# Compression weights split by VectorE, and the compression's steps moved in the filler list of a hybrid attention block

## The chip, the cores and the metric

One core of one Trainium2 chip runs the whole program. The metric is device time in microseconds from launch to end. Three runs of the kernel before gave 636.03, 636.63 and 637.7 us; the median is 636.63 us.

Five engines work in parallel, each through its own instructions in order: TensorE (PE; its weight loads are shown as PEld), VectorE (DVE), ScalarE (ACT), GpSimd (POOL), and SyncE (SP), which here only starts transfers. An instruction that waits holds up all that stands behind it on its engine.

## The reference

The input x is 512 tokens by 1024. The block does, in this order:

- h = rms_norm(x); u = h @ w_in. The columns of u are queries, three pairs of keys and values, head gates, and three times 512 columns for a gated convolution (b, c, x_t).
- Attention of 8 heads (2 groups) in three branches. For the compressed one, windows of 32 keys (values) at stride 16 go through a two-layer network: `gelu(blk @ w1) @ w2`, 31 compressed keys and values per group. The other two branches are the selected blocks and the sliding window. Each branch has a bias, a softmax and a gate.
- A convolution branch: b * dwconv3(c * x_t).
- Both are joined, multiplied by w_out, normed and added to x. A gated MLP with a width-3 convolution (2 x 2816 columns up, 2816 rows down) follows in the same way.

All of it is float32.

## The kernel before

**Exact products from two halves.** Every operand X of a large matmul is kept as hi = X rounded to the matmul's type, and lo = X - hi. A product takes three matmuls: hi*hi, hi*lo, lo*hi (`mm3`, L169). For the weights, `Stream._split` makes both halves: ACT copies the raw tile to hi (L85), another engine subtracts to get lo (L88). That engine is DVE, except for the tiles named in `pool_lo`: there it is POOL, in four pieces of 256 columns (L81 to L88). Before, `pool_lo` holds the eight tiles `c1_0` to `c1_7`, the weights of the compression's first layer (L167).

**The weight stream.** Weight tiles of 128 x 1024 come in one fixed order, that in which the filler list first names them. Raw tiles have three buffers: a load waits until the raw tile three places earlier has been split. Split tiles have four buffers (`ringp`, L119): the hi copy of a tile waits until TensorE has used the tile four places earlier for the last time. Splits carry a raised priority (L96).

**The filler list.** After the startup, TensorE's work is of two sorts. One is attention, in 14 parts (`Part`: scores, exp, transposes, products with the values), each of which needs DVE and ACT between its matmuls. The other is filler, which needs no softmax: `ORDER` (L44) is a list of steps, and `fill(n)` takes the next n steps of it. The names: `c`, `q` are projections for compressed keys/values and queries; `h0` to `h7` are the first layer of the compression (two steps each: 16 matmuls of 256 columns, weight `c1_n`); `s` is `second_layer` in three steps (L462); `g`, `x`, `b` with 0 to 3 are the convolution's three projections of one 128-channel tile, eight steps of three 512-column matmuls each. So `g0:2` is two steps of gate projection 0.

**What sets the counts.** All filler up to the last `s` step (`PRE2`, L154) is placed ahead of the first attention part's second half, because the compressed scores (`pcs`) need the second layer's result. What is left (`TOTAL - PRE2`) is spread over the twelve parts that follow (L711). The framework's scheduler then orders each engine's instructions by priority and readiness, so the order on an engine is not that of the source.

**The second layer**, step one: ACT copies half of the accumulator `ph` to `g1` (L467), DVE adds the other half (L468). Step two: TensorE transposes `g1` into `pg` (L472), ACT applies gelu to get `GT`, which needs a table load (L481), DVE copies it to `GV`. Step three: TensorE multiplies by `w2` (`pc`, `pvc`), the results are split to `KC` and `VC`, and `KC` is copied to the other partitions by a transfer.

**A convolution tile**: g gives `cz` (DVE), x multiplies it (DVE, L532), POOL scales it (two pieces, L519), POOL and DVE apply the three taps to get `ct` (L535, L537), POOL scales again (L519), b multiplies (DVE, L544), and ACT and DVE split it into `oTc` (L134, L135).

Of the kernel before, what the change touches and what calls it, by code (L numbers as in the profile page):

```python
# [40 lines left out]
BIG = 1e30  # L41


ORDER = ("c0 c1 q2 q3:4 h0 q3:4 h1 g0:2 h2 g0:2 h3 g0:2 h4 g0:2 h5 x0:4 h6 x0:4 h7 s:1 b0:3 s:1 b0:3 s:1 b0:2 "  # L44
         "g1 x1 b1 g2 x2 b2 g3 x3 b3")
LOADS = "g w", "T0 T1 T2 w T3 T4 b T5 w T6 T7 w", "x0 x1 v x2 x3 w"
T_TILES = 20
WARM = 8
# [62 lines left out]
def block_kernel(ctx: ExitStack, tc: tile.TileContext, a, out):  # L111
# [28 lines left out]
    c1 = lambda c: (a["w_c1"][c].rearrange("p l c -> p (l c)"), 1024, f"c1_{c}")  # L140
# [7 lines left out]
    order = []  # L148
    for what in ORDER.split():
        name, _, count = what.partition(":")  # L150
# [13 lines left out]
    items += [(a["w_d"][f * P:(f + 1) * P, :], 1024, f"d{f}") for f in range(NF)]  # L164
    W = Stream(tc, nc, rawp, ringp, items, loads=0)
    W.pieces["v0"] = 280
    W.pool_lo |= {f"c1_{c}" for c in range(8)}  # L167

    def mm3(dst, wh, wl, xh, xl, first, last):  # L169
        MM(dst, wh, xh, start=first, stop=False)  # L170
# [583 lines left out]
    x1 = late.tile([P, NT, D], F32, name="x1")  # L754
# [104 lines left out]
    for n, m in enumerate(UP):  # L859
# [7 lines left out]
        if m >= NF:  # L867
            f = m - NF
# [97 lines left out]
```

## Time and profile before

| | |
|---|---|
| median of three runs | 636.63 us |
| profiled execution, its own time | 636.99 us |
| its span, first to last instruction | 635.2 us |
| TensorE busy | 622.5 us (98%) |
| VectorE / ScalarE / GpSimd busy | 368.4 / 306.3 / 71.7 us |
| mean granted TensorE clock | 0.992 of 2.4 GHz |

The page's own note says that a busy TensorE is not one at its peak: matmuls overlap in the pipeline, so the start of one to the start of the next is the pace, not the duration shown. The program has four stretches: startup up to some 43 us, filler and the first part to about 113 us, attention with filler to about 222 us, and then the output projection and the MLP.

### The profile page before, as it was taken

The page shows a single profiled execution, that of the slowest core. Times are in us where ns is not written, and L with a number is a line of the kernel's source. Part 1 is how long each engine was busy: PE and PEld are TensorE (multiplying, and loading weights), DVE is VectorE, ACT ScalarE, POOL GpSimd, SP SyncE. Part 2 cuts the span into 40 slices and gives each one's busy share as a digit, 9 for nine tenths or more (in the row PEclk, how much of TensorE's full clock was granted, in tenths as well). Part 3 has the DMA queues.
Part 4 walks back from the last instruction along what each step waited for, and adds up shares of the span by engine and source line. Part 5 has one row for each costly group of instructions (what it writes and reads, how often), then busy time and mean ns, then how long its engine had stood idle before and what let it go on. Part 6 is the DMA issues. An engine that isn't in the chain of part 4 may idle for free.

```text
span 635.2 us, 8091 instructions
## 1 busy us (share of the span) xinstructions
PE 622.5 (98%) x2980; PEld 518.7 (82%) x2980; DVE 368.4 (58%) x657; ACT 306.3 (48%) x562; POOL 71.7 (11%) x122
## 2 busy tenths in 40 slices
PE   8999997999999999999999999999999999999996
PEld 7888895888878788898888888888888888888884
DVE  5686625799978756638665656565656642222225
ACT  6666634789878744436343444444444422222212
POOL 1204383002230302200000000000000000000001
PEclk9999997999999999999999999999999999999998
DMA  8876455111121474004233233322222232232203
GB/s 324 322 208 185 130 180 166 43 43 42 42 76 42 152 269 165 11 1 135 99 99 101 99 100 99 101 100 98 90 88 96 93 111 92 97 100 99 67 0 133
DMA packets 26294, 71.44 MB, mean 112 GB/s; under 512 B 3368, under 2 KB 8040, under 8 KB 26256
## 3 DMA queue, kind: packets, MB, share of 16 engines
q1 hardware_dynamic: 25968, 70.65, 33.6%
q8 instruction: 23, 0.38, 0.2%
q10 hardware_dynamic: 288, 0.29, 0.1%
q14 instruction: 15, 0.12, 0.1%
HBM read 64.88 MB, written 2.12 MB: 105 GB/s over the span
## 4 chain that ended last, share of the span: by engine, by line
PE 82%; DMA 5%; DVE 4%; ACT 3%; POOL 3%; issue 2%; SPq 1%; DVEq 0%; POOLq 0%; ACTq 0%
PE pu L171 13%; PE pu L170 13%; PE pu L172 13%; PE z L770 6%; PE z L772 6%; PE z L771 6%; PE tr L650 3%; PE sc L621 2%; PE y L772 2%; PE y L770 2%; PE y L771 2%; POOL w_c L88 2%; DMA raw_tb<-in_w_t 2%; PE o L658 2%; PE o L659 1%
## 5 line engine op out<-in xcount | busy, mean ns | idle before, releaser
L170 PE MATMUL pu<-h2T,w_u 128*128 128x512 f32 (+1 forms) x384 | 142.8, 372 | 0.0
L171 PE MATMUL pu<-h2T,w_u 128*128 128x512 f32 (+1 forms) x384 | 142.6, 371 | 0.0
L172 PE MATMUL pu<-h2T,w_u 128*128 128x512 f32 (+1 forms) x384 | 142.6, 371 | 0.0
L170 PEld LDWEIGHTS pu<-h2T,w_u 128*128 128x128 f32 x384 | 72.4, 188 | 12.6
L172 PEld LDWEIGHTS pu<-h2T,w_u 128*128 128x128 f32 x384 | 72.3, 188 | 12.5
L171 PEld LDWEIGHTS pu<-h2T,w_u 128*128 128x128 f32 x384 | 72.4, 188 | 12.3
L854 DVE SCALAR_TENSOR_TENSOR cv<-pu,ffnw,cv 128x511 f32<-128x511 f32 x44 | 32.9, 749 | 70.2 <-ACT cv L853 70.2
L88 DVE TENSOR_TENSOR w_d<-raw_d,w_d 128x1024 fp32r<-128x1024 f32 x22 | 26.9, 1224 | 72.8 <-ACT w_d L85 72.8
L771 PE MATMUL z<-w_d,aT 128*128 128x512 f32 x176 | 68.5, 389 | 0.0
L770 PE MATMUL z<-w_d,aT 128*128 128x512 f32 x176 | 68.5, 389 | 0.0
L772 PE MATMUL z<-w_d,aT 128*128 128x512 f32 x176 | 68.5, 389 | 0.0
L853 ACT ACTIVATE cv<-pu,ffnw 128x512 f32<-128x512 f32 x44 | 30.3, 688 | 63.7 <-PE pu L172 63.6
L85 ACT ACTIVATE w_d<-raw_d 128x1024 fp32r<-128x1024 f32 x22 | 23.3, 1059 | 75.2 <-PE z L772 75.2
L88 DVE TENSOR_TENSOR w_u<-raw_u,w_u 128x1024 fp32r<-128x1024 f32 x44 | 53.4, 1216 | 5.8 <-ACT w_u L85 5.8
L85 ACT ACTIVATE w_u<-raw_u 128x1024 fp32r<-128x1024 f32 x44 | 46.2, 1052 | 6.5 <-PE pu L172 6.3
L254 POOL TENSOR_SCALAR rsz<-ssz 128x1 f32<-128x1 f32 x4 | 1.2, 300 | 355.0 <-ACT jz L893 355.0
L627 ACT ACTIVATE P<-P,mins 128x512 f32<-128x512 f32 (+3 forms) x64 | 35.4, 555 | 10.1 <-DVE mins L625 9.7
L772 PEld LDWEIGHTS z<-w_d,aT 128*128 128x128 f32 x176 | 33.0, 188 | 6.9
L771 PEld LDWEIGHTS z<-w_d,aT 128*128 128x128 f32 x176 | 33.0, 188 | 6.9
L770 PEld LDWEIGHTS z<-w_d,aT 128*128 128x128 f32 x176 | 33.0, 188 | 6.8
L134 ACT ACTIVATE aT<-cv 128x512 fp32r<-128x512 f32 x22 | 13.9, 632 | 49.5 <-DVE cv L871 49.5
L855 DVE SCALAR_TENSOR_TENSOR cv<-pu,ffnw,cv 128x510 f32<-128x510 f32 x44 | 32.8, 748 | 1.5
(222 smaller groups left out, 1165.0 us busy)
## 6 DMA issues: line engine op xcount, KB each, us to landing
raw_u<-in_w_u SPq DMA_DIRECT2D x44, 512.0 KB, 3.2
raw_d<-in_w_d SPq DMA_DIRECT2D x22, 512.0 KB, 3.2
raw_c<-in_w_c SPq DMA_DIRECT2D x8, 512.0 KB, 3.4
raw_o<-in_w_o SPq DMA_DIRECT2D x8, 512.0 KB, 3.3
xT<-in_xT SPq DMA_DIRECT2D x8, 256.0 KB, 5.4
xt<-in_x SPq DMA_DIRECT2D x4, 512.0 KB, 5.9
raw_q<-in_w_t SPq DMA_DIRECT2D x4, 512.0 KB, 6.6
UR<-vd SPq DMA_DIRECT2D x2, 1024.0 KB, 8.7
```

Source lines behind the costliest of these rows:

```text
L85: self.nc.scalar.activation(t[:, 0, c:c + step], self.raws[n][:, c:c + step], AF.Copy)
L88: eng.tensor_tensor(t[:, 1, cs], self.raws[n][:, cs], f32(t[:, 0, cs]), op=ALU.subtract)
L170: MM(dst, wh, xh, start=first, stop=False)
L171: MM(dst, wh, xl, start=False, stop=False)
L172: MM(dst, wl, xh, start=False, stop=last)
L627: act(v, v, AF.Exp, bias=m, scale=-1.0, accum_out=self.sums[:, r, b:b + 1])
L770: MM(y, oh_, w[:, 0, cs], start=first, stop=False)
L771: MM(y, ol_, w[:, 0, cs], start=False, stop=False)
L772: MM(y, oh_, w[:, 1, cs], start=False, stop=last)
L853: act(t, pu, AF.Copy, scale=ffnw[:, m, 2:3])
L854: nc.vector.scalar_tensor_tensor(t[:, 1:], pu[:, :S - 1], ffnw[:, m, 1:2], t[:, 1:], op0=ALU.mult, op1=ALU.add)
L855: nc.vector.scalar_tensor_tensor(t[:, 2:], pu[:, :S - 2], ffnw[:, m, 0:1], t[:, 2:], op0=ALU.mult, op1=ALU.add)
```

## The change

`c1_0` to `c1_7` are no longer in `pool_lo`, so their lo halves are made by DVE, in one instruction of 1024 columns each instead of four POOL instructions of 256. And `ORDER` is rewritten: the first layer's `h2` to `h7` stand four projection steps apart each (before: two steps apart for `h2` to `h5`, then four), with `g0`, `x0` and all of `b0` between them; and the second layer's three steps stand between steps of `g1` (before: of `b0`). The second layer comes after 82 list steps instead of 73, so the twelve parts that follow share 65 steps instead of 74.

```diff
@@ -41,8 +41,8 @@
-ORDER = ("c0 c1 q2 q3:4 h0 q3:4 h1 g0:2 h2 g0:2 h3 g0:2 h4 g0:2 h5 x0:4 h6 x0:4 h7 s:1 b0:3 s:1 b0:3 s:1 b0:2 "
-         "g1 x1 b1 g2 x2 b2 g3 x3 b3")
+ORDER = ("c0 c1 q2 q3:4 h0 q3:4 h1 g0:4 h2 g0:4 h3 x0:4 h4 x0:4 h5 b0:4 h6 b0:4 h7 s:1 g1:4 s:1 g1:3 s:1 g1:1 "
+         "x1 b1 g2 x2 b2 g3 x3 b3")
@@ -164,7 +164,6 @@
     W.pieces["v0"] = 280
-    W.pool_lo |= {f"c1_{c}" for c in range(8)}
```

One line less stands ahead of most of the code, so line numbers after the change are one smaller.

ScalarE, where the second layer begins, before: the hi copies of the next weights (`w_tg1`, `w_tx1`, `w_tb1` are gate, x and b of channel tile 1), then the copy to `g1`.

```order
L85 ACTIVATE w_c1_7_934<-raw_c1_7_877 128x1024
L85 ACTIVATE w_tb0_954<-raw_tb0_896 128x1024
L85 ACTIVATE w_tg1_988<-raw_tg1_923 128x1024
L85 ACTIVATE w_tx1_1007<-raw_tx1_940 128x1024
L85 ACTIVATE w_tb1_1276<-raw_tb1_957 128x1024
L467 ACTIVATE g1_1003<-ph_759 64x512
L481 ACT_TABLE_LOAD
L481 ACTIVATE GT_1026<-pg_1021,peb_1028 128x2x31 x4
```

The same place on ScalarE after the change:

```order
L85 ACTIVATE w_c1_7_952<-raw_c1_7_888 128x1024
L85 ACTIVATE w_tg1_969<-raw_tg1_905 128x1024
L85 ACTIVATE w_tx1_997<-raw_tx1_941 128x1024
L85 ACTIVATE w_tb1_1016<-raw_tb1_955 128x1024
L134 ACTIVATE oTc_511<-ct0_932 128x512
L466 ACTIVATE g1_1012<-ph_753 64x512
L85 ACTIVATE w_tg2_1279<-raw_tg2_972 128x1024
L480 ACT_TABLE_LOAD
L480 ACTIVATE GT_1038<-pg_1033,peb_1040 128x2x31 x4
```

The copy to `g1` still stands behind the hi copies of `w_tx1` and `w_tb1`, and now also behind the split of the finished convolution tile 0.

VectorE at the same place, before:

```order
L88 TENSOR_TENSOR w_tx1_1007<-raw_tx1_940,w_tx1_1007 128x1024
L537 SCALAR_TENSOR_TENSOR ct0_982<-cz0_914,convw_290,ct0_982 128x512
L468 TENSOR_TENSOR g1_1003<-ph_759,g1_1003 64x512
L537 SCALAR_TENSOR_TENSOR ct0_982<-cz0_914,convw_290,ct0_982 128x512
L478 COPY peb_1028<-pg_1021 128x4
```

And after:

```order
L88 TENSOR_TENSOR w_c1_7_952<-raw_c1_7_888,w_c1_7_952 128x1024
L88 TENSOR_TENSOR w_tg1_969<-raw_tg1_905,w_tg1_969 128x1024
L536 SCALAR_TENSOR_TENSOR ct0_932<-cz0_868,convw_290,ct0_932 128x512 x2
L88 TENSOR_TENSOR w_tx1_997<-raw_tx1_941,w_tx1_997 128x1024
L543 TENSOR_TENSOR ct0_932<-pbg0_951,ct0_932 128x512
L88 TENSOR_TENSOR w_tb1_1016<-raw_tb1_955,w_tb1_1016 128x1024
L135 TENSOR_TENSOR oTc_511<-ct0_932,oTc_511 128x512
L467 TENSOR_TENSOR g1_1012<-ph_753,g1_1012 64x512
```

Ahead of the addition to `g1` now stand the product with b0 (L543), the lo half of `w_tb1` and that of `oTc`. On TensorE, the transposes `pg` of `g1` stood behind `h7` and 13 matmuls of `b0`; now they stand behind `h7` and 12 matmuls of `g1`.

## Rows read from the trace of the kernel before

**Rows 1.** The page: the span, and busy time, share and instructions of each engine.

```profile
span 635.2 us, 8091 instructions
PE 622.5 (98%) x2980; PEld 518.7 (82%) x2980; DVE 368.4 (58%) x657; ACT 306.3 (48%) x562; POOL 71.7 (11%) x122
```

**Rows 2.** TensorE's waits, 0 to 260 us: total, times, longest, us.

```profile
PE pg L472 <- DVE g L468: 3.9, 1, 3.9
```

**Rows 3.** TensorE in order of time: start us, us, [idle before].

```profile
87.72 0.39 PE L170 MATMUL pxt<-hT,w_tx 128*128 128x512 f32 x1
...
90.48 1.84 PE L458 MATMUL ph<-w_c,X 128*128 128x256 f32 x8
92.16 0.40 PE L170 MATMUL pxt<-hT,w_tx 128*128 128x512 f32 x1
...
99.29 0.39 PE L170 MATMUL pbg<-hT,w_tb 128*128 128x512 f32 x1
103.56 0.69 PE L472 MATMUL pg<-ident,g 64*128 64x64 f32 x4 [3.88 <-DVE g L468]
```

**Rows 4.** Stretches of 2 us: busy of PE, PEld, DVE, ACT, POOL; clock; DMA.

```profile
102.00:104.00 2.00, 0.44 (x4) 0.45 (x4) 1.18 (x2) 1.96 (x3) 0.00 (x0) 0.64 0.49 186
104.00:106.00 2.00, 2.00 (x7) 1.54 (x6) 1.88 (x4) 1.01 (x5) 1.69 (x2) 0.50 0.01 2
106.00:108.00 2.00, 2.00 (x6) 1.32 (x4) 1.06 (x2) 0.00 (x0) 0.91 (x2) 0.50 0.62 213
108.00:110.00 2.00, 2.00 (x7) 1.07 (x7) 0.00 (x0) 0.20 (x1) 0.00 (x0) 0.66 0.12 49
```

**Rows 5.** ScalarE in order of time, ahead of the second layer.

```profile
101.11 1.06 ACT L85 ACTIVATE w_tb<-raw_tb 128x1024 fp32r<-128x1024 f32 x1 [2.11 <-DMA raw_tb<-in_w_t]
102.19 0.59 ACT L467 ACTIVATE g<-ph 64x512 f32<-64x512 f32 x1
```

**Rows 6.** VectorE in order of time, the same place.

```profile
93.81 1.83 DVE L88 TENSOR_TENSOR w_tb<-raw_tb,w_tb 128x1024 fp32r<-128x1024 f32 x1 [6.81 <-ACT w_tb L85]
...
97.19 0.68 DVE L532 TENSOR_TENSOR cz<-pxt,cz 128x512 f32<-128x512 f32 x1
99.03 1.24 DVE L88 TENSOR_TENSOR w_tx<-raw_tx,w_tx 128x1024 fp32r<-128x1024 f32 x1 [1.16 <-ACT w_tx L85]
100.87 0.75 DVE L537 SCALAR_TENSOR_TENSOR ct<-cz,convw,ct 128x512 f32<-128x512 f32 x1 [0.59 <-POOL ct L535]
102.82 0.68 DVE L468 TENSOR_TENSOR g<-ph,g 64x512 f32<-64x512 f32 x1 [1.20 <-ACT g L467]
...
104.36 1.22 DVE L88 TENSOR_TENSOR w_tb<-raw_tb,w_tb 128x1024 fp32r<-128x1024 f32 x1
```

**Rows 7.** GpSimd in order of time, the same place.

```profile
91.74 2.82 POOL L88 TENSOR_TENSOR w_c<-raw_c,w_c 128x256 fp32r<-128x256 f32 x4 [1.12 <-ACT w_c L85]
97.95 1.24 POOL L519 TENSOR_TENSOR cz<-cz,Rb 128x256 f32<-128x256 f32 x2 [3.39 <-DVE cz L532]
99.29 1.54 POOL L535 TENSOR_SCALAR ct<-cz,convw 128x512 f32<-128x512 f32 x1
...
104.38 2.54 POOL L519 TENSOR_TENSOR ct<-ct,Rb 128x256 f32<-128x256 f32 x2
```

**Rows 8.** Tile oTc, 90 to 135 us: duration ns min/median/max, starts.

```profile
L135 DVE TENSOR_TENSOR oTc<-ct,oTc x1: 678/678/678, 132.8 to 132.8; 128x512 fp32r<-128x512 f32 x1
```

**Rows 9.** The DMA queue's waits, 40 to 115 us: total, times, longest, us.

```profile
SPq L73 <- POOL w_c L88: 20.7, 7, 3.4
```

**Rows 10.** Stretches, columns as in rows 4.

```profile
70.00:100.00 30.00, 29.68 (x135) 26.65 (x133) 11.52 (x14) 14.25 (x17) 20.77 (x28) 1.00 0.51 165
113.30:169.50 56.20, 56.19 (x314) 46.16 (x313) 50.22 (x153) 50.12 (x117) 9.18 (x15) 1.00 0.13 38
169.50:222.20 52.70, 51.96 (x269) 41.53 (x268) 41.48 (x138) 40.59 (x119) 13.68 (x20) 1.00 0.28 90
141.60:156.70 15.10, 15.10 (x83) 12.51 (x82) 13.30 (x40) 14.04 (x35) 3.30 (x6) 1.00 0.15 45
```

## The prediction, made before the changed kernel ran

> **What bounds the kernel now.** I read the page first: TensorE is busy 622.5 of 635.2 us [rows 1]. So only time in which it stands, or runs slowly, can be won, and work that merely changes place wins nothing. TensorE's waits come next. From the start to the end of attention there is one that matters: 3.9 us in one piece, where the transposes `pg` wait for DVE's addition to `g1` [rows 2]. In order of time, TensorE's last matmul ahead of it runs from 99.29 to 99.68 us, and it goes on at 103.56 [rows 3]. ScalarE shows why: the copy to `g1` (102.19) stood behind the hi copy of a weight (`w_tb1`), which waited for its transfer until 101.11 [rows 5]. The addition then ran from 102.82 to 103.50 [rows 6]. TensorE had nothing in its order to do meanwhile.
>
> The stretches around the gap show a second loss. The granted clock is 0.64 in 102 to 104, 0.50 in the next two, 0.66 in 108 to 110 [rows 4]. At 0.5 that is (1-0.64)*2/0.5 = 1.44, 4.0 and 1.36 us, together 6.8 us at 1.2 GHz. It begins at 104-1.44 = 102.56, still in the gap, and TensorE works from 103.56, so 5.8 us of work ran at half speed and cost 2.9 us. The place costs 3.9 + 2.9 = 6.8 us.
>
> **Part one: lo of the eight tiles on DVE.** POOL loses 32 pieces; four took 2.82 us [rows 7]. DVE gains 8 instructions like that of 99.03 or 104.36, 1.22 to 1.24 us [rows 6]: 9.8 us. Two fall near 52 and 58 us; six in the stretch 70 to 100, where DVE is busy 11.52 of 30 us [rows 10]. With 7.4 more it has 18.9, so the cover is there, and I cost it at nothing; without cover it would be at most the 9.8. The raw buffer comes free earlier (2.82 against 1.24 us); the loads had waited seven times, 20.7 us in all, for POOL's lo [rows 9]. TensorE waited for none of these, so that too gains nothing directly, but it makes weights earlier where ScalarE waited for one.
>
> **Part two: the place of the second layer.** I follow the new order from S, the start of the last matmul of b0. TensorE's next one starts 0.23 us later (12 projection matmuls take 90.48 - 87.72 = 2.76 us, the eight of an `h` 92.16 - 90.48 = 1.68 [rows 3]). `h7` and 12 of g1 bring it to `pg` at S + 0.23 + 1.68 + 2.76 = S + 4.7.
>
> The other side: `w_tx1` takes the ring buffer of b0's weight, four places earlier, so its hi copy waits for b0's end: S + 0.39 [rows 3]. Then, on ACT and DVE in turn: hi copy 1.06 [rows 5], lo 1.24 [rows 6], product with b0 0.68 (as at 97.19), lo of `w_tb1` 1.22, lo of `oTc` 0.68 [rows 8], addition 0.68. ScalarE's split of `oTc` and copy to `g1` lie beside the lo of `w_tb1`. Sum 5.95, with handoffs some 6.1: `pg` waits 6.1 - 4.7 = 1.4 us.
>
> That is the lower end. The upper comes from tile 0's convolution, which must be done before the product. From the end of L532 (97.87) to POOL's last piece (106.92) it took 9.05 us [rows 6, 7], with waits of its own. In the new order L532 comes after x0's end and after hi and lo of `h6` (0.39 + 1.06 + 1.24 + 0.68 = 3.4 after the last x0 matmul starts). b0's last one starts 2*1.68 + 2*2.76 = 8.9 after that, so 9.05 us of convolution end at S + 3.55, against S + 2.7 for the lo of `w_tx1`: 0.9 later. So `pg` waits 1.4 to 2.3 us; I take 1.8. Behind `pg` stand only matmuls of g1 and x1, so a wait there delays everything.
>
> GpSimd's last two pieces at 104.38 took 2.54 us, just as DVE's lo of 1.22 us ran, and DVE's lo at 93.81 took 1.83, where a POOL piece was running until 94.56 [rows 6, 7]. The Trainium skill ("SBUF — State Buffer", section "Who interferes with whom") says why: a DVE instruction with two SBUF inputs and a GpSimd instruction that reads SBUF exclude each other, and the second blocks until the first is done. The trace agrees: 94.56 plus about 1.1 is the end at 95.64. It speaks against this change at one place: DVE's own lo work now lies beside tile 0's convolution on POOL. By that rule the upper end, 2.3, would hold, and the sum would be 0.5 us more.
>
> The clock: it fell 2.9 us after TensorE stopped, in a stop of 3.9 us. No row has a stop of 1.4 to 2.3 us, so the price is between 0 and 2.9 us again; I take 0, since the row's fall came later than such a stop would end.
>
> After `pg`, the chain to `KC` and the compressed scores has 12 matmuls of g1 and 22 of x1 for cover (7.8 us), against gelu, a weight's hi and lo, and a transfer; I cost it at nothing.
>
> **Part three: less filler in attention.** Before the compressed scores TensorE now has 118 projection matmuls of the convolution instead of 82: 36 * 0.23 = 8.3 us of filler left the attention phase. Total TensorE work is the same, so this costs only what the phase stalls more. Between the ends of the eight head-group pieces the fillers go from 19, 15, 23, 21, 35, 45, 24, 24 to 24, 12, 23, 15, 22, 32, 25, 17. First four pieces (113.3 to 169.5): 4 fewer, 0.9 us; the list shows ScalarE one hi copy more: 50.12 + 1.06 = 51.2 us of ACT in 55.3, 93% where it was 89% [rows 10]. Last four: 32 fewer, 7.4 us, and two hi copies fewer: 38.5 in 45.3, 85% where it was 77%.
>
> Lower end 0: in 141.6 to 156.7 ScalarE was busy 14.04 of 15.1 us, 93%, and TensorE did not stand [rows 10]. Upper end: ACT keeps the shares it had, 51.2/0.89 = 57.4 and 38.5/0.77 = 50.0, 2.1 and 4.7 us more, 6.8 in all. I take 1.7, a quarter of the way, nearer to the row of the tight piece, since neither half goes above its share.
>
> **The sum**, against the profiled execution's own 636.99 us (0.36 above the median): -3.9 - 2.9 + 1.8 + 1.7 = -3.3, so 633.7; by the median 633.3 us.
>
> **Rivals.**
> - *Everything pays.* The wait is at its lower end, attention stalls no more, and a little is won elsewhere by earlier weights: 636.63 - 6.8 + 1.4 = 631.2, at best some 630.5. For it: 93% of ACT without a stop. Against it: convolution and lo share DVE and POOL just before `pg`.
> - *ScalarE sets the pace of attention.* About 4.4 of the 6.8 us come back: 636.63 - 6.8 + 1.8 + 4.4 = 636.0. For it: the first hi copy there (`w_tb2`) stands ahead of the first exp of the next part, and it waits for x1's last matmul. Against: the last four pieces have ample ACT time.
> - *The clock falls again* in the wait at `pg`: 633.3 + 2.9 = 636.2. For it: no row shows such a stop; against: the time to the fall above.
> - *Slower: attention keeps its length.* If its 108.9 us are set by the latency from score to exp to transpose to product, and the filler only fits in between, then the 8.3 us moved ahead are paid in full: 633.3 - 1.7 + 8.3 = 639.9. It decides from 5.2 us of extra stall on. Against: TensorE is busy 56.19 of 56.2 and 51.96 of 52.7 us there.
> - *That DVE does not make lo* can be left out: the order shows it does.
>
> **How the numbers follow.** Chances: forecast 57% (own range 631.7 to 635.3), everything pays 12%, ScalarE's pace 14%, clock 8%, attention keeps its length 9%. A measurement of this kernel tells 0.3%, 1.9 us, from no change: faster means below 634.7, slower above 638.5. Faster: 0.12 and about 0.49 of the forecast's 0.57, 0.61. Slower: the last rival and a little, 0.10. The rest, 0.29, is the same. The range from 630.3 to 637.2 takes in all cases but the last and half the tail of the first.
>
> **What would show it.** Right: TensorE's wait for `g1` falls to 1.4 to 2.3 us, the clock stays at 1.0 from 60 us on, POOL shows no `w_c`, and from the compressed scores to the last attention product it takes 100 to 103 us instead of 108.9. Wrong: a wait at `h4` to `h7` for a lo from DVE; a clock of 0.5 after `pg`; or an attention phase above 106 us with ACT above 90%.

## The result and the profile after

The changed kernel took 632.6 us (median of five runs, 632.26 to 633.81), the kernel before 636.72 us beside it; the ratio is 0.9932, interval 0.9914 to 0.995. Run once more later it took 632.08 us (ratio 0.9906, 0.9886 to 0.9926). The forecast was 633.3 us, in a range from 630.3 to 637.2: faster, as forecast.

First the page of the changed kernel: span, then busy time, share and instructions by engine.

```profile
span 632.0 us, 8054 instructions
PE 622.0 (98%) x2980; PEld 517.8 (82%) x2980; DVE 372.9 (59%) x665; ACT 305.3 (48%) x562; POOL 42.8 (7%) x90
```

Against [rows 1] TensorE's work is the same, GpSimd has lost 29 us and VectorE gained 4.5. That is less than the 9.8 us that eight lo halves take, so other VectorE instructions became shorter, some 5.4 us in all: the four subtractions for `tails` went from 1.9 to 0.6 us and the two copies to `GV` from 1.6 to 0.5. All of these ran beside GpSimd's pieces before, and none does now. TensorE's waits to 260 us follow (total, times, longest, us):

```profile
PE wu L197 <- DVE first L234: 1.4, 1, 1.4
PE pv L299 <- ACT w_v L85: 0.6, 1, 0.6
PE tr L649 <- POOL P L638: 0.3, 1, 0.3
PE o L677 <- DMA bd<-zt: 0.2, 1, 0.2
PE tr L649 <- ACT P L640: 0.2, 1, 0.2
```

The row for `pg` of [rows 2] is gone. In order of time, TensorE goes from `h7` (101.23) through 12 matmuls of g1 to `pg` and to the scores without a stop:

```profile
101.00 0.40 PE L171 MATMUL pbg<-hT,w_tb 128*128 128x512 f32 x1
101.23 1.83 PE L457 MATMUL ph<-w_c,X 128*128 128x256 f32 x8
...
105.73 0.46 PE L471 MATMUL pg<-ident,g 64*128 64x64 f32 x4
...
116.78 0.98 PE L574 MATMUL pcs<-KC,Q 128*128 128x64 f32 x8
```

The granted clock stays at 1.00 around it, where [rows 4] had 0.64 and 0.50 (stretch; busy of PE, PEld, DVE, ACT, POOL; clock; DMA):

```profile
104.00:106.00 2.00, 2.00 (x12) 1.41 (x11) 2.00 (x3) 1.93 (x2) 0.00 (x0) 1.00 0.66 217
106.00:108.00 2.00, 2.00 (x11) 1.63 (x10) 0.74 (x4) 0.92 (x4) 0.00 (x0) 1.00 0.60 186
```

ScalarE and then VectorE ahead of the second layer, beside [rows 5, 6]:

```profile
98.69 1.06 ACT L85 ACTIVATE w_tx<-raw_tx 128x1024 fp32r<-128x1024 f32 x1 [3.38 <-PE ph L457]
101.44 1.06 ACT L85 ACTIVATE w_tb<-raw_tb 128x1024 fp32r<-128x1024 f32 x1 [1.68 <-PE pbg L171]
102.40 0.61 ACT L134 ACTIVATE oTc<-ct 128x512 fp32r<-128x512 f32 x1
103.10 0.60 ACT L466 ACTIVATE g<-ph 64x512 f32<-64x512 f32 x1
```

```profile
99.79 1.62 DVE L88 TENSOR_TENSOR w_tx<-raw_tx,w_tx 128x1024 fp32r<-128x1024 f32 x1 [0.98 <-ACT w_tx L85]
101.49 0.69 DVE L543 TENSOR_TENSOR ct<-pbg,ct 128x512 f32<-128x512 f32 x1
102.53 1.22 DVE L88 TENSOR_TENSOR w_tb<-raw_tb,w_tb 128x1024 fp32r<-128x1024 f32 x1 [0.35 <-ACT w_tb L85]
103.67 0.68 DVE L135 TENSOR_TENSOR oTc<-ct,oTc 128x512 fp32r<-128x512 f32 x1
104.27 0.68 DVE L467 TENSOR_TENSOR g<-ph,g 64x512 f32<-64x512 f32 x1
```

ScalarE no longer waits for a transfer here: both hi copies wait for TensorE, that is, for a free buffer. `w_tx1` starts when `h6` is done (96.82 + 1.84 = 98.66), `w_tb1` when b0 is done (101.00 + 0.40). The addition ends at 104.95, 0.8 us before TensorE gets to `pg`.

The attention phase in two halves, as [rows 10] has it for before:

```profile
116.80:173.20 56.40, 56.20 (x310) 45.57 (x309) 50.82 (x158) 49.72 (x117) 8.40 (x16) 1.00 0.14 39
173.20:218.30 45.10, 44.63 (x236) 35.35 (x235) 37.96 (x133) 38.12 (x116) 9.68 (x18) 1.00 0.25 79
```

56.2 and 52.7 us have become 56.4 and 45.1. So the 9.0 us of work that left the phase (8.2 of filler, and 0.8 of transposes and value products that now stand ahead of the scores) shortened it by 7.4.

### The profile page after: what moved, and what is told of

It is laid out like the page before. It is cut to its first block, busy times and chain, and to the rows that moved or that the text cites. A ratio compares the mean times of both kernels' runs of the same rounds, so it can differ in the third digit from the quotient of the medians.

```text
span 632.0 us, 8054 instructions
## 1 busy us (share of the span) xinstructions
PE 622.0 (98%) x2980; PEld 517.8 (82%) x2980; DVE 372.9 (59%) x665; ACT 305.3 (48%) x562; POOL 42.8 (7%) x90
## 4 chain that ended last, share of the span: by engine, by line
PE 94%; DVE 2%; DMA 1%; ACT 1%; POOL 0%; SPq 0%; issue 0%; DVEq 0%; POOLq 0%; ACTq 0%
PE pu L170 13%; PE pu L171 13%; PE pu L169 13%; PE z L770 6%; PE z L769 6%; PE z L771 6%; PE sc L620 3%; PE y L770 2%; PE y L771 2%; PE y L769 2%; PE tr L649 2%; PE ph L457 2%; PE o L657 1%; PE o L658 1%; PE pcg L169 1%; PE pcg L171 1%
## 5 line engine op out<-in xcount | busy, mean ns | idle before, releaser
L85 ACT ACTIVATE w_u<-raw_u 128x1024 fp32r<-128x1024 f32 x44 | 46.2, 1052 | 6.6 <-PE pu L171 6.3
L624 DVE CUSTOM_DVE_ANT_0 P<-sc,UR 128x512 f32<-128x512 f32 (+3 forms) x64 | 30.1, 482 | 2.6 <-PE sc L620 1.7
```

The lines of the kernel that those rows point to most:

```text
L85: self.nc.scalar.activation(t[:, 0, c:c + step], self.raws[n][:, c:c + step], AF.Copy)
```

## The experiments

In these runs theory A says: the stop at `pg` and the low clock behind it are all there is to win, and filler taken out of attention is paid for by more stalls there. The rivals are named in the expectations. The kernel before ran beside each set; its own runs scatter by some us (636.1 to 642.2 beside e1 to e4, median 637.91; 637.6 beside the others), so a kernel is compared by its ratio, or with one that ran beside it. The expectations count from 636.7.

**e1_lo_alone: the first part of the change alone.**

```diff
-    W.pool_lo |= {f"c1_{c}" for c in range(8)}
```

> Part one alone: lo of the eight compression tiles on VectorE, the old filler list. Theory A (all there is to win is TensorE's stop at pg, 3.9 us, and the half clock behind it, 2.9 us; both come from the weight w_tb1 arriving late on ScalarE ahead of the copy to g1, and earlier raw buffers cure that): no wait at pg, clock 1.0 throughout, the 82 filler matmuls ahead of the compressed scores as before, so nothing is given back: 636.7 - 6.8 = 629.9 us. Rival B (the new place of the second layer is what removes the wait, the engine of lo is a side matter): the wait stays, 636 to 637 us.

Measured: 632.17 us, ratio 0.9899 (0.9864 to 0.9934): 5.7 us less, where theory A wanted 6.8. The profiled run's waits from 60 us to the end of attention:

```profile
PE tr L649 <- ACT P L640: 0.7, 1, 0.7
PE pg L471 <- DVE g L467: 0.6, 1, 0.6
```

The old filler list is not what made TensorE stop: with lo on VectorE it stops for 0.6 us instead of 3.9, and the clock stays at 1.00. The hi copy of `w_tb1` no longer waits for a transfer:

```profile
96.46 1.07 ACT L85 ACTIVATE w_tb<-raw_tb 128x1024 fp32r<-128x1024 f32 x1 [0.60 <-PE ph L457]
97.55 0.59 ACT L466 ACTIVATE g<-ph 64x512 f32<-64x512 f32 x1
```

Its load began sooner, as the expectation said: first the row before, then that of e1.

```profile
95.67 0.33 SPq L73 DMA_DIRECT2D raw_tb<-in_w_t  x1
89.95 0.33 SPq L73 DMA_DIRECT2D raw_tb<-in_w_t  x1
```

Rival B falls. The sum of the queue's waits would not have told it: in e1 the loads wait for VectorE's lo nearly as long, 20.1 us in eight, as they did for GpSimd's [rows 9].

**e2_order_alone: the second part alone**, the new `ORDER` with `pool_lo` kept.

> Part two alone: the new filler list, lo of the compression tiles still on GpSimd. Theory A: raw tiles are in time here too since the first layer's steps stand wider apart, but tile 0's convolution on GpSimd now queues with the last lo pieces, so the copy to g1 is late by 0 to 1.5 us: 632.6 to 634.1 us, clock 1.0. Rival B: as the whole change, 632.6 us. Rival C (only lo on VectorE cures the stop): the stop of 3 to 4 us and the low clock stay and the filler moved ahead is paid: 637 to 639 us.

Measured: 634.04 us, ratio 0.9926 (0.9898 to 0.9955). TensorE's wait, and the stretch in which it stands:

```profile
PE pg L472 <- DVE g L468: 1.9, 1, 1.9
```

```profile
106.00:108.00 2.00, 0.23 (x1) 0.00 (x0) 2.00 (x4) 1.96 (x4) 0.00 (x0) 1.00 0.41 115
108.00:110.00 2.00, 1.90 (x11) 1.57 (x12) 1.28 (x3) 1.94 (x5) 0.00 (x0) 1.00 0.64 242
```

GpSimd, the load of `w_tb1`, ScalarE and VectorE show where the 1.9 us come from:

```profile
96.50 3.82 POOL L88 TENSOR_TENSOR w_c<-raw_c,w_c 128x256 fp32r<-128x256 f32 x4 [0.93 <-ACT w_c L85]
100.30 0.69 POOL L535 TENSOR_SCALAR ct<-cz,convw 128x512 f32<-128x512 f32 x1
102.64 2.35 POOL L519 TENSOR_TENSOR ct<-ct,Rb 128x256 f32<-128x256 f32 x2 [1.66 <-DVE ct L537]
```

```profile
100.34 0.33 SPq L73 DMA_DIRECT2D raw_tb<-in_w_t  x1
104.34 1.06 ACT L85 ACTIVATE w_tb<-raw_tb 128x1024 fp32r<-128x1024 f32 x1 [4.10 <-DMA raw_tb<-in_w_t]
105.03 0.69 DVE L544 TENSOR_TENSOR ct<-pbg,ct 128x512 f32<-128x512 f32 x1 [1.33 <-POOL ct L519]
105.64 1.22 DVE L88 TENSOR_TENSOR w_tb<-raw_tb,w_tb 128x1024 fp32r<-128x1024 f32 x1
```

The last lo pieces of `c1_7` (96.50 to 100.32) hold up two things. Tile 0's convolution on GpSimd is late, and the product with b0 waits for it. And the load of `w_tb1` begins only as they end, so its hi copy waits for the transfer as in the kernel before, and ends at 105.40. Its lo half, at 105.64, could have begun at most some 0.2 us sooner without the convolution. So the late transfer alone accounts for about 1.7 of the 1.9 us; the convolution runs nearly level with it.

Either part alone thus removes most of the 6.8 us: part one takes away the late transfer, part two leaves it, with a shorter stop behind which the clock stays at 1.00. Rival C falls by its time, though GpSimd's lo, which it names, causes what is left of the stop. With both parts nothing of it is left.

**e3_s_in_g1: only the second layer moved.**

```diff
-... h7 s:1 b0:3 s:1 b0:3 s:1 b0:2 g1 x1 b1 ...
+... h7 b0 s:1 g1:4 s:1 g1:3 s:1 g1:1 x1 b1 ...
```

> Only the second layer is moved: all of b0 and then its steps between those of g1, the first layer's steps spaced as before, lo on GpSimd. TensorE has 36 matmuls (8.2 us) between h7 and pg instead of 13. Theory A: the stop is covered, 6.8 us won, 24 matmuls moved out of attention cost about 1.1 (1.7 for 36): 631.0 us. Rival C: w_tb1 is late all the same and the stop moves along: 635 to 637 us.

Measured: 633.32 us (631.17 to 637.66 in twelve runs), ratio 0.9929 (0.9906 to 0.9953). That is 2.3 us over the 631.0 expected, and 1.1 too little by the difference to the kernel before: 36 matmuls did not cover the wait.

```profile
PE pg L472 <- DVE g L468: 2.1, 1, 2.1
PE pc L487 <- ACT GT L481: 1.2, 1, 1.2
```

```profile
102.62 1.06 ACT L85 ACTIVATE w_tx<-raw_tx 128x1024 fp32r<-128x1024 f32 x1 [6.25 <-DMA raw_tx<-in_w_t]
```

The hi copies again wait for a transfer, here that of `w_tx1`: the stop is in part moved along, as rival C had it, and a second one stands behind it at the gelu. In this profile the clock stayed at 1.00 through both.

**e4_s_in_b0: the changed kernel with fewer steps ahead of the scores.**

```diff
-... x0:4 h4 x0:4 h5 b0:4 h6 b0:4 h7 s:1 g1:4 s:1 g1:3 s:1 g1:1 x1 ...
+... x0:2 h4 x0:2 h5 x0:2 h6 x0:2 h7 s:1 b0:4 s:1 b0:3 s:1 b0:1 g1 x1 ...
```

> The changed kernel with less filler ahead of the compressed scores: h4 to h7 two steps apart, the second layer between steps of b0, lo on VectorE. 94 convolution matmuls ahead of the scores instead of 118 (82 before). Theory A: no wait at pg, and 24 fewer moved give back two thirds of the 1.7 us: 631.5 us. Rival D (the filler moved ahead costs nothing, the attention phase is as dense): 632.6 us. Rival E (each moved step is paid in full, 0.23 us a matmul): 627 us.

Measured: 633.0 us, ratio 0.9915 (0.9883 to 0.9946), between the two ratios of the whole change (0.9932 and 0.9906): no difference is shown. Rival E falls; theory A and rival D are not told apart. There is a wait where none was expected, and one in attention:

```profile
PE pg L471 <- DVE g L467: 1.0, 1, 1.0
PE o L658 <- DVE ptl L135: 0.8, 1, 0.8
```

From the scores to the last attention product it took 111.07 to 218.11, 107.0 us, where 12 moved matmuls (2.7 us), and some 0.5 us of transposes and a value product that stand ahead of the scores here, should leave 105.4 of the 108.7 before. So 12 moved matmuls go with 1.6 us of stall. In e3 24 moved ones go with some 0.4 (116.72 to 220.38, 103.7 us, where 103.3 should be left). The stall does not follow the number of moved steps.

**whole_again and lo_alone_again: the whole change and part one, side by side.**

> The whole change once more, beside part one alone on the same chip. Theory A with what the first runs showed (the stop is gone in both; moved filler makes attention stall 1 to 1.7 us more): 4 to 5 us under the kernel before, and 0.4 to 1.5 us over part one alone.

> Part one alone once more. Theory A: 5 to 6.5 us under the kernel before, 0.4 to 1.5 us under the whole change. Rival D (the filler list neither gains nor loses): equal to the whole change within 0.3 us.

Measured: whole 632.08 us (631.79 to 633.32), part one alone 631.39 us (631.36 to 631.5); ratios 0.9906 (0.9886 to 0.9926) and 0.9894 (0.9875 to 0.9914). The whole change won 5.5 us, just over the 4 to 5 expected; part one alone won 6.2, as expected. The two sets of runs don't overlap, though the intervals, wide from the scatter of the kernel before, do. Where attention begins and ends on TensorE, first scores and last product, first in the profile of e1_lo_alone, then in that of whole_again:

```profile
107.19 1.06 PE L574 MATMUL pcs<-KC,Q 128*128 128x64 f32 x8
216.01 0.44 PE L677 MATMUL o<-bd,VC 128*128 128x512 f32 x1
```

```profile
115.95 0.98 PE L574 MATMUL pcs<-KC,Q 128*128 128x64 f32 x8
217.64 0.39 PE L677 MATMUL o<-bd,VC 128*128 128x512 f32 x1
```

Part one alone keeps attention at 108.8 us, as before. The whole change has it at 101.7, with 9.0 us less to do: 1.9 us of new stall (1.6 in the first profile, against the kernel before). The new filler list thus costs more than the 0.6 us of stop that it removes, by 0.7 us in the medians. In the earlier set part one alone scattered more (631.25 to 633.16), so the size of that 0.7 is not settled.

**g2_x0_split: no stop, and the old amount of filler.** Lo on VectorE, and, against the list of the kernel before,

```diff
-... h5 x0:4 h6 x0:4 h7 s:1 b0:3 s:1 b0:3 s:1 b0:2 ...
+... h5 x0:2 h6 x0:2 h7 x0:2 s:1 x0:2 b0:2 s:1 b0:3 s:1 b0:3 ...
```

> Lo on VectorE, h6 and h7 two steps apart, the second layer's first two steps between the last steps of x0 and b0: 18 matmuls cover pg instead of 13, and the addition to g1 stands on VectorE ahead of tile 0's convolution taps, behind which part one alone waited 0.6 us. 81 filler matmuls ahead of the scores (82 in part one alone). Theory A: no wait at pg, 0.6 us under part one alone. Rival: the wait moves to the gelu or to the weights x1 and b1: equal or worse.

Measured: 631.09 us (630.87 to 631.83), ratio 0.9891 (0.9871 to 0.9911): the best of all, 1.0 us under the whole change. The 0.6 us under part one alone that theory A wanted are not shown: it is 0.3, and the runs overlap. `pg` has no wait. The addition stands ahead of the convolution and ends at 95.1; TensorE gets to `pg` at 97.81.

```profile
94.45 0.68 DVE L467 TENSOR_TENSOR g<-ph,g 64x512 f32<-64x512 f32 x1 [1.35 <-ACT g L466]
100.38 0.75 DVE L536 SCALAR_TENSOR_TENSOR ct<-cz,convw,ct 128x512 f32<-128x512 f32 x1 [1.33 <-POOL ct L534]
```

**g3_less_ahead: still less filler ahead** (as g2 up to `h7`, then `s:1 x0:4 s:1 b0:3 s:1 b0:5`; 70 matmuls ahead of the scores).

> As the one before, but the second layer between x0's and b0's steps so that only 70 matmuls stand ahead of the scores and 12 cover pg. If less filler in attention costs stalls, more filler (12 matmuls more) gains: attention from scores to the last product stalls up to 0.5 us less, but with 12 for cover pg may wait 0 to 1 us: within 0.6 us of part one alone.

Measured: 633.96 us, ratio 0.9935 (0.9918 to 0.9952), 2.6 us over part one alone, against an expectation of at most 0.6. TensorE waits in many places:

```profile
PE pvc L492 <- DVE GV L482: 1.0, 1, 1.0
PE o L657 <- DVE fin L688: 0.6, 1, 0.6
PE tr L649 <- DVE ptl L135: 0.6, 1, 0.6
PE sc L620 <- DVE mins L624: 0.4, 1, 0.4
```

Attention took 112.4 us (106.11 to 218.49), 3.6 more than in part one alone for 2.7 us more filler: more filler did not make it denser. Three more of its transposes stand ahead of the scores, so the stall is some 1.1 us. Another 1.3 us or so were lost ahead of the scores, where `pc` waited 0.4 and `pvc` 1.0 us. With e3 and e4 this speaks against a price per moved step.

## Why the prediction was right, and where it was off

**The 6.8 us at `pg`: right in kind, 0.4 too much.** Both pieces went, in the profile of the changed kernel in full: from the first `ph` to the scores it took 67.10 to 113.28 before and 68.01 to 116.78 after, 46.2 and 48.8 us, with 9.0 us more work in it, so 6.4 us were won. Part one alone, with the 0.6 us stop, won 5.8 in that place. The difference to 6.8 lies in the clock's share: from `pg` to the scores the same matmuls took 9.7 us before (103.56 to 113.28) and 7.2 in e1 (100.02 to 107.19), so the low clock cost 2.6 us and not 2.9.

**Part one, costed at nothing: wrong as a price of its own.** The prediction saw that it makes weights earlier "where ScalarE waited for one", but gave the gain to the new place of the second layer. With part one alone (e1) the late transfer, and with it 5.8 of the 6.4 us, is gone; the waits of the raw loads were on TensorE's path after all.

**The wait that was to stay, 1.4 to 2.3 us, taken as 1.8: wrong; it measured none.** The step that failed is that `w_tx1` "takes the ring buffer of b0's weight, four places earlier". Its hi copy started at 98.69, at `h6`'s end, 2.7 us before b0's. The split buffers are not handed on four places later, as the description of the weight stream has it, but in the order in which they come free: `h6`'s weight was named after b0's but used up before it, in the new list alone. The hi copy of `h4`'s weight (80.99, at `h2`'s end, with g0's weight, four places earlier, in use until 83.70) shows the same. So `w_tx1` was split by 101.41, and only `w_tb1` and `oTc` stood between b0's end and the addition: 1.06 + 1.22 + 0.68 + 0.68 with the addition itself, less the overlap of neighbours, 101.44 to 104.95. The product with b0 ran beside the hi copy. The other half of that step, tile 0's convolution on GpSimd, was also put too late: 93.28 to 100.33, 7.05 us instead of 9.05, and it set out 1.1 us after x0's last matmul began instead of 3.4, as it did not have to wait for the split of `h6`'s weight. So it was done before b0's end. In e2, where GpSimd still made lo, that chain and the late transfer together cost 1.9 us.

**The shared port.** GpSimd's pieces at 93.36 and 98.89 took 2.23 and 1.44 us for two, where two with VectorE idle took 1.24 (97.95 in [rows 7]). Beside them the lo halves on VectorE took 1.40 and 1.62 us, where 1.22 is the time alone:

```profile
93.36 2.23 POOL L518 TENSOR_TENSOR cz<-cz,Rb 128x256 f32<-128x256 f32 x2 [23.26 <-DVE cz L531]
98.89 1.44 POOL L518 TENSOR_TENSOR ct<-ct,Rb 128x256 f32<-128x256 f32 x2 [1.66 <-DVE ct L536]
```

The rule of the Trainium skill ("SBUF — State Buffer", "Who interferes with whom") was borne out as a mechanism; the upper end that it was to bring did not come, since the product (101.49) followed b0's end and the lo of `w_tx1`, and not GpSimd, which was done at 100.33.

**The clock: 0 came true, since no wait was left**, so the changed kernel did not test the price. e2 and e3 did: in their profiles TensorE stood 1.9 and 2.1 us with the clock at 1.00 through and after, against a fall in the stop of 3.9 us. These are single executions. All seven runs of e2 have a mean clock of 0.996 or more, but one of the twelve of e3 has 0.992, as the kernel before in its profile, and took 637.66 us. So that a stop of this length costs no clock is shown for two executions, not in general.

**Attention's stalls, taken as 1.7 us: right in size** (1.6 and 1.9 in two profiles), wrong in place. By halves, 54.5 us of work took 56.4 (1.9 of stall, near the upper end of 2.1 given for that half), and 45.3 took 45.1 (none of the 4.7). The halves don't hold quite the work that was counted: four score matmuls, some 0.5 us, that stood in the second half run in the first now (60 instead of 56), so the stalls are nearer 1.4 and 0.3. The first half is where ScalarE was said to be tight, at 93%; but it was busy 49.72 of 56.4 us there, 88%, and not the 51.2 that were counted. Over the whole of attention, the wait of TensorE's weight loads for ScalarE's copies of the transposed tile grew from 2.3 us in nine to this:

```profile
PEld o L657 <- ACT pth L134: 3.6, 14, 0.4
```

It grew in both halves, from 1.2 to 1.6 and from 1.1 to 1.9 us, and more in the one that stalls less. So that the stall comes from ScalarE's share is not shown, and these rows speak against it: e4 and g3 stall by 1.6 and 1.1 us with more filler. What the experiments show is that a changed order there cost from 0.4 (e3) to 1.9 us; its cause is open.

**The sum.** With what the profiles show, -6.4 + 0 and 1.6 to 1.9 make -4.8 to -4.5, against a measured -4.1 (interval -5.5 to -3.2) and -5.5 in the second set of runs. The forecast of -3.3 held a wait of 1.8 that did not come and 0.4 of gain too much. That 633.3 lies so near to 632.6 is in part luck: the two errors go opposite ways, and the kernel before alone scatters by more than what is left. Of "everything pays", the lowest wait came, and more than that, but the dense attention did not; the attention rivals, the clock and the slower case did not come.

**Of the two parts**, the first carries the gain: 631.39 us alone, 632.08 with the second.

## What to carry to other kernels

An engine that finishes its own instructions in time can still be what stops another one, through the buffers it holds: no matmul waited for one of GpSimd's lo halves, but these kept raw buffers full, a load late and a copy on ScalarE behind it. So follow a stop back through the buffers before moving work around it, and try the parts of a change one by one; here the part that looked like the cure gave part of the gain back. And where a pool's buffers don't come free in the order of naming, ask which comes free first.

## What was not expected of the hardware

In both profiled runs of the whole change one of the eight output transfers at the end took longer to land, and the last matmul starts 7.7 us ahead of the end, against 6.6 before and 6.9 in part one alone (median and largest, us, of the output's transfers; the first row is before, the second the whole change):

```profile
DMA to landing us min/median/max: 2.0/2.0/2.3
```

```profile
DMA to landing us min/median/max: 2.0/2.0/3.1
```

The profiled executions of the whole change (633.81 and 633.32 us) are 1.2 us above their medians, so this 1.1 us may belong to profiled executions, though those of the other kernels with lo on VectorE don't show it; its cause is open. It is the reason why medians, and not spans, stand in the comparison of the two parts.
